# Output projection of a hybrid decoder layer: seven products per 2x2 by 2x2 of tiles in place of eight

## Chip, cores and metric

The kernel runs on one NeuronCore of a Trainium2 chip. The metric is the device time of one execution in microseconds, median of several executions. Engines are named as in the profile: PE (TensorE matmul), PEld (TensorE weight load), DVE (VectorE), ACT (ScalarE), POOL (GpSimd), SP (SyncE, which here issues most loads).

## The reference

One layer on x of 256 tokens by 4096 channels, float32. The change touches the last line but one alone, `merged @ w_out`, a product of 256x4096 by 4096x4096.

```python
h = rms_norm(x, norm_gains[l])
z = h @ w_in[l]                       # all projections at once
...                                   # gated linear attention -> o_a, window attention -> o_b
y_a = (o_a * silu(gg)) @ w_gla_out[l]
y_b = (o_b * silu(sg)) @ w_swa_out[l]
merged = sigmoid(ga + b_gates[l, 0]) * y_a + sigmoid(gb + b_gates[l, 1]) * y_b
x = x + merged @ w_out[l]
...
return rms_norm(x, final_norm_gain)
```

## The kernel before, in words

All large products have one form, the helper `gemm`. The 256 tokens are two tiles (t = 0, 1) of 128 and lie, transposed, as the stationary side; the weights stream as the moving side in blocks of 512 columns; the contraction runs over tiles of 128 rows (KT = 32 of them for 4096). To come near float32, each side is split into a high part, rounded to the type float32r, and a low part, the rest, and three float32r products are added in PSUM: high by high (L136), high by low (L137), low by high (L138). A chunk of two contraction tiles (KW = 2) is one load of 512 KB on SP's queue (L148, `raw`, four buffers), one cast on ScalarE (L154, `hi`) and one subtraction on VectorE (L155, `lo`), both 128x1024, with three buffers each. Then come 12 matmuls (two contraction tiles, two token tiles, three products).

The stages follow each other: the attention branches, `ya` (GLA output projection), eight rounds of the gates `ga`, `gb` and the projection `yb` with the merge into the array `ya`, and last the output projection in eight blocks `o0` to `o7` of 512 columns, with residual, squares for the final norm, and gain. Its stationary side `mT` is `ya` transposed on TensorE (`transpose_split`, L184, tiles `m_t`) and split by ScalarE (L174) and VectorE (L175). Seven of its eight parts are transposed ahead of the last `yb`, the eighth inside `o0`.

Tile pools give out the buffers, and a scheduler lays the instructions of each engine in a fixed order when the kernel is built; the preparation of weights stands in `high_priority`, so it is laid ahead of other work. Each engine runs its order strictly, and waits at an instruction whose inputs or buffers aren't ready.

## Time and profile before

| what | value |
|---|---|
| median of 3 runs | 2497.19 us (2496.21 to 2499.42) |
| span of the profiled execution | 2494.7 us |
| lowest and highest run above that span | 1.5 and 4.7 us |
| PE busy share of the span | 99% |
| VectorE busy share | 52% |
| ScalarE busy share | 44% |
| HBM traffic over the span | 189 GB/s |

The span is what the profiler saw from the first to the last instruction of one execution; the median lies 2.5 us above it. Shares are means over the whole span. The output projection alone is the stretch from 2134.8 to 2484.0 us.

### The profile page before, as it was taken

To read this page: it belongs to the slowest core of one execution; us is meant where nothing else is said; L and a number is where in the kernel's file an instruction comes from. 1 tells how busy PE (TensorE), PEld (TensorE's weight loads), DVE (VectorE), ACT (ScalarE), POOL (GpSimd) and SP (SyncE) were. 2 spreads that over 40 slices of the span, in tenths; PEclk is the share of its full clock that TensorE was granted. 3 is DMA by queue.
4 is the path that set the end of the run, shared out by engine and by line. 5 is a ranking of instruction groups with operands and counts; after the bars stand their busy time and mean duration, and the time that the engine had idled before them with its cause. 6 is when DMAs were issued, how large, how long until landed. Compare 5 with 4: busy or idle time off the path is not lost.

```text
span 2494.7 us, 28744 instructions
## 1 busy us (share of the span) xinstructions
PE 2469.9 (99%) x11220; PEld 2033.3 (82%) x11220; DVE 1306.1 (52%) x1303; ACT 1093.1 (44%) x1289; POOL 41.4 (2%) x52
## 2 busy tenths in 40 slices
PE   8999999999999999999999999999999999999998
PEld 6788888888888888888888888888888888888886
DVE  8565555545444455555555454555545456544544
ACT  6444444434444444544444444444444444444443
POOL 4000000000000000000000000000000000000000
PEclk9999999999999999999999999999999999999999
DMA  7455555445555545454465556665666555665655
GB/s 258 156 175 188 170 175 195 175 168 188 194 192 195 193 148 193 150 171 166 150 211 199 198 198 197 197 202 197 198 196 198 194 194 177 236 211 203 211 203 186
DMA packets 132985, 474.32 MB, mean 190 GB/s; under 512 B 15056, under 2 KB 15440, under 8 KB 132720
## 3 DMA queue, kind: packets, MB, share of 16 engines
q1 hardware_dynamic: 127584, 461.69, 54.5%
q10 hardware_dynamic: 5264, 10.79, 1.4%
q8 instruction: 88, 1.44, 0.2%
q14 instruction: 49, 0.40, 0.0%
HBM read 468.23 MB, written 4.19 MB: 189 GB/s over the span
## 4 chain that ended last, share of the span: by engine, by line
PE 95%; DVE 2%; issue 1%; ACT 1%; DMA 0%; POOL 0%; SPq 0%; ACTq 0%; POOLq 0%; DVEq 0%
PE ga_a L137 5%; PE ga_a L136 5%; PE gb_a L137 5%; PE gb_a L136 5%; PE ga_a L138 5%; PE gb_a L138 5%; PE o_a L136 5%; PE o_a L137 5%; PE o_a L138 5%; PE sg_a L137 2%; PE sg_a L136 2%; PE sg_a L138 2%; PE sq_a L138 2%; PE sq_a L137 2%; PE ya_a L136 2%; PE ya_a L137 2%
## 5 line engine op out<-in xcount | busy, mean ns | idle before, releaser
L155 DVE TENSOR_TENSOR ga_l<-ga_r,ga_h 128x1024 fp32r<-128x1024 f32 x128 | 156.8, 1225 | 171.6 <-ACT ga_h L154 171.6
L155 DVE TENSOR_TENSOR gb_l<-gb_r,gb_h 128x1024 fp32r<-128x1024 f32 x128 | 156.9, 1225 | 171.1 <-ACT gb_h L154 171.1
L155 DVE TENSOR_TENSOR o_l<-o_r,o_h 128x1024 fp32r<-128x1024 f32 x124 | 152.0, 1225 | 161.4 <-ACT o_h L154 161.3
L154 ACT CAST ga_h<-ga_r 128x1024 fp32r<-128x1024 f32 x128 | 135.2, 1057 | 209.8 <-PE ga_a L138 171.5
L154 ACT CAST gb_h<-gb_r 128x1024 fp32r<-128x1024 f32 x128 | 135.2, 1056 | 204.5 <-PE gb_a L138 159.4
L154 ACT CAST o_h<-o_r 128x1024 fp32r<-128x1024 f32 x124 | 131.0, 1056 | 193.2 <-PE o_a L138 186.2
L138 PE MATMUL ga_a<-ga_h,hT 128*128 128x512 f32 x512 | 199.4, 389 | 0.0
L137 PE MATMUL ga_a<-ga_l,hT 128*128 128x512 f32 x512 | 199.2, 389 | 0.0
L136 PE MATMUL ga_a<-ga_h,hT 128*128 128x512 f32 x512 | 199.2, 389 | 0.0
L138 PE MATMUL gb_a<-gb_h,hT 128*128 128x512 f32 x512 | 199.2, 389 | 0.0
L136 PE MATMUL gb_a<-gb_h,hT 128*128 128x512 f32 x512 | 199.2, 389 | 0.0
L137 PE MATMUL gb_a<-gb_l,hT 128*128 128x512 f32 x512 | 199.2, 389 | 0.0
L138 PE MATMUL o_a<-o_h,mT 128*128 128x512 f32 x496 | 193.0, 389 | 0.0
L137 PE MATMUL o_a<-o_l,mT 128*128 128x512 f32 x496 | 193.0, 389 | 0.0
L136 PE MATMUL o_a<-o_h,mT 128*128 128x512 f32 x496 | 192.9, 389 | 0.0
L155 DVE TENSOR_TENSOR ya_l<-ya_r,ya_h 128x1024 fp32r<-128x1024 f32 x64 | 78.4, 1226 | 95.6 <-ACT ya_h L154 95.6
L155 DVE TENSOR_TENSOR sq_l<-sq_r,sq_h 128x1024 fp32r<-128x1024 f32 x64 | 78.4, 1225 | 84.8 <-ACT sq_h L154 84.8
L155 DVE TENSOR_TENSOR yb_l<-yb_r,yb_h 128x1024 fp32r<-128x1024 f32 x64 | 78.4, 1225 | 82.8 <-ACT yb_h L154 82.8
L155 DVE TENSOR_TENSOR gg_l<-gg_r,gg_h 128x1024 fp32r<-128x1024 f32 x64 | 78.3, 1224 | 75.9 <-ACT gg_h L154 75.9
L155 DVE TENSOR_TENSOR sg_l<-sg_r,sg_h 128x1024 fp32r<-128x1024 f32 x64 | 78.3, 1223 | 72.7 <-ACT sg_h L154 72.7
L154 ACT CAST sg_h<-sg_r 128x1024 fp32r<-128x1024 f32 x64 | 67.4, 1053 | 111.0 <-PE sg_a L138 94.7
L155 DVE TENSOR_TENSOR gv_l<-gv_r,gv_h 128x1024 fp32r<-128x1024 f32 x64 | 78.2, 1224 | 67.9 <-ACT gv_h L154 67.9
(278 smaller groups left out, 5568.3 us busy)
## 6 DMA issues: line engine op xcount, KB each, us to landing
ga_r<-in_win_dram SPq DMA_DIRECT2D x128, 512.0 KB, 4.3
gb_r<-in_win_dram SPq DMA_DIRECT2D x128, 512.0 KB, 4.2
o_r<-in_wout_dram SPq DMA_DIRECT2D x128, 512.0 KB, 3.3
gv_r<-in_win_dram SPq DMA_DIRECT2D x64, 512.0 KB, 3.2
gg_r<-in_win_dram SPq DMA_DIRECT2D x64, 512.0 KB, 3.3
ya_r<-in_wgla_dram SPq DMA_DIRECT2D x64, 512.0 KB, 3.2
sq_r<-in_win_dram SPq DMA_DIRECT2D x64, 512.0 KB, 3.2
sg_r<-in_win_dram SPq DMA_DIRECT2D x64, 512.0 KB, 3.3
```

Source lines behind the costliest of these rows:

```text
L136: nc.tensor.matmul(acc[t], lh, hi[:, i, :], start=kt == 0, stop=False)
L137: nc.tensor.matmul(acc[t], lh, lo[:, i, :], start=False, stop=False)
L138: nc.tensor.matmul(acc[t], ll, hi[:, i, :], start=False, stop=kt == nkt - 1)
L154: nc.scalar.copy(hi, raw)
L155: nc.vector.tensor_tensor(lo, raw, hi.bitcast(F32), ALU.subtract)
```

## The change

The output projection is computed by the scheme of seven products (Winograd's form of Strassen's). One unit, numbered j = 0 to 15 within a block, takes two contraction tiles, two token tiles and two blocks of 512 columns at once, so there are four blocks of 1024 columns (named `o0`, `o2`, `o4`, `o6` in the code) of 16 units each. One load of 1 MB (L569, `raw`, two buffers) brings the four weight tiles of a unit, laid out for it by the host. Of the seven products of a unit three (q1, q2, q3) are one plain float32 matmul each, with the unsplit tiles on both sides (L602); the other four are three float32r matmuls each (L598 to L600) on sums of weight tiles. The sums are made on VectorE (L571, 128x1024 into `t13`; L589 and L590, 128x512 into `t24`), split by ScalarE (L578) and VectorE (L579), 128x1024 for each pair. The seven results gather over the 16 units in seven PSUM banks and are combined by VectorE at the block's end (L630 to L637), followed by residual, squares and gain (L622 within `done`).

The transposes of `ya` all move behind the last `yb`: `combine(j)` transposes four 128x128 tiles into the eighth PSUM bank (one buffer, `tp`), ScalarE copies them out, VectorE makes four sums of 128x128 (L552 to L555), ScalarE casts and VectorE subtracts 128x512 (L557, L558). The pools of the earlier stages are closed first, and the new tiles lie where those tiles lay.

```diff
 STG = 3
+NFULL = 3
+T13 = 1
+BUFS = {"13": 2, "24": 2}
...
-            if n == NBLK - 1:
-                mT = big.tile([P, KT, 2, S], F32R, tag="hT", name="mT")
-                for m in range(n):
-                    merged(m)
...
-        for n in range(NBLK):
-            cs = slice(n * NB, (n + 1) * NB)
-            xt = fp.tile([P, NT, NB], F32, tag="xt", name=f"xt{n}", bufs=2)
...
-            acc = gemm(
-                f"o{n}", mT, wout[n], KT,
-                before=(lambda k0, _: merged(NBLK - 1) if k0 == 8 else None) if n == 0 else None,
-                trail=STG + 4 if n == NBLK - 1 else 0, hold=hold,
-            )
...
+    early.close()
...
+    def combine(j):
...
+        tp = qps.tile([P, 512], F32, tag="tp", name=f"m_t{j}")
+        for k in range(2):
             for t in range(NT):
...
+                nc.tensor.transpose(tp[:, k * S + t * P : k * S + (t + 1) * P], ya[:, t, c : c + P], ident)
+        tv = tp.rearrange("p (k t c) -> p k t c", k=2, t=NT)
+        cs = fp.tile([P, 6, P], F32, tag="cs", name=f"cs{j}", bufs=2)
+        nc.scalar.copy(fl[:, 0:2, :], tv[:, :, 0, :])
+        nc.scalar.copy(cs[:, 0:2, :], tv[:, :, 1, :])
...
+        nc.vector.tensor_tensor(cs[:, 2, :], cs[:, 0, :], cs[:, 1, :], ALU.subtract)
+        nc.vector.tensor_tensor(cs[:, 4, :], fl[:, 0, :], cs[:, 0, :], ALU.subtract)
+        nc.vector.tensor_tensor(cs[:, 3, :], cs[:, 2, :], fl[:, 0, :], ALU.subtract)
+        nc.vector.tensor_tensor(s4, fl[:, 1, :], cs[:, 3, :], ALU.add)
+        c = cs[:, 1 : 8 - NFULL, :]
+        nc.scalar.copy(sp_[:, :, 0, :], c)
+        nc.vector.tensor_tensor(sp_[:, :, 1, :], c, sp_[:, :, 0, :].bitcast(F32), ALU.subtract)
...
+    def sevens(name, w, npr):
...
+        q = {i: qps.tile([P, NB], F32, tag=f"q{i}", name=f"{name}_q{i}") for i in range(1, 8)}
+        for j in range(npr):
+            with tc.high_priority(PRIO):
+                raw = wp.tile([P, 4, NB], F32, tag="raw", name=f"{name}_r{j}", bufs=2)
+                nc.sync.dma_start(raw, w[j])
+                t13 = wp.tile([P, 2, NB], F32, tag="t13", name=f"{name}_t{j}", bufs=T13)
+                nc.vector.tensor_tensor(
+                    t13, raw[:, 0:2, :], raw[:, 2:3, :].broadcast_to([P, 2, NB]), ALU.add
+                )
...
+                    nc.scalar.copy(hi, src)
+                    nc.vector.tensor_tensor(lo, src, hi.bitcast(F32), ALU.subtract)
...
+                t24 = wp.tile([P, 2, NB], F32, tag="t24", name=f"{name}_s{j}")
+                nc.vector.tensor_tensor(t24[:, 0, :], t13[:, 1, :], raw[:, 0, :], ALU.add)
+                nc.vector.tensor_tensor(t24[:, 1, :], t24[:, 0, :], raw[:, 3, :], ALU.add)
...
+            order = (1, 6, 5, 3, 2, 7, 4) if j == npr - 1 else (1, 2, 3, 5, 7, 6, 4)
...
+                    nc.tensor.matmul(q[i], l[:, 0, :], hi, start=st, stop=False)
+                    nc.tensor.matmul(q[i], l[:, 0, :], lo, start=False, stop=False)
+                    nc.tensor.matmul(q[i], l[:, 1, :], hi, start=False, stop=sp_)
+                else:
+                    nc.tensor.matmul(q[i], full[j // GRP][:, j % GRP, FULL[i], :], right[i], start=st, stop=sp_)
...
+        nc.scalar.copy(u, q[1])
+        add(v, q[6], u)
+        add(y, q[5], v, ALU.subtract)
+        add(x2[:, 0, cs[1]], q[3], y)
+        add(x2[:, 0, cs[0]], q[2], u)
+        add(w, q[7], v)
+        add(x2[:, 1, cs[1]], q[5], w, ALU.subtract)
+        add(x2[:, 1, cs[0]], q[4], w)
+        for t, i in ((0, 1), (0, 0), (1, 1), (1, 0)):
+            done(t, i)
```

What the build lays on the engines, at the places that the prediction speaks of. First TensorE at the end of the last `yb` (L136 to L138 before, L140 to L142 now), where the output projection begins. Before:

```order
L136 MATMUL yb_a_15026<-yb_h_15155,obT 128x512
L137 MATMUL yb_a_15026<-yb_l_15156,obT 128x512
L138 MATMUL yb_a_15026<-yb_h_15155,obT 128x512
L136 MATMUL o_a_15185<-o_h_15189,mT 128x512
L137 MATMUL o_a_15185<-o_l_15190,mT 128x512
```

And now, at the same place:

```order
L140 MATMUL yb_a_14927<-yb_h_15056,obT 128x512
L141 MATMUL yb_a_14927<-yb_l_15057,obT 128x512
L142 MATMUL yb_a_14927<-yb_h_15056,obT 128x512
L546 MATMUL m_t_15103<-ident,ya 128x128 x4
L546 MATMUL m_t_15117<-ident,ya 128x128 x4
L546 MATMUL m_t_15131<-ident,ya 128x128 x4
L602 MATMUL o_q_15331<-o_r_15338,full_15093 128x512
```

Three of the sixteen groups of transposes now stand between the last `yb` and the first product; the others are strewn over the first block. The first two loads of the output projection on SP's queue, with the semaphores that they wait for, before and now:

```order
L148 DMA o_r_15187<-in_wout_dram 128x1024 [waits DMAHW6_49,DVE_49]
L148 DMA o_r_15205<-in_wout_dram 128x1024 [waits DMAHW7_49,DVE_49]
```

```order
L569 DMA o_r_15338<-in_wout_dram 128x2048 [waits PE_49]
L569 DMA o_r_15368<-in_wout_dram 128x2048 [waits DMAHW1_49,DMAHW0_49,DVE_49]
```

The first load waited for VectorE's use of a staging buffer; now it waits for TensorE, to a count that the last matmul of the last `yb` reaches, since its tile lies where `obT` lay. Second, VectorE in the middle of a block, before (the whole preparation of three chunks is three rows):

```order
L155 TENSOR_TENSOR o_l_16224<-o_r_16221,o_h_16223 128x1024
L155 TENSOR_TENSOR o_l_16242<-o_r_16239,o_h_16241 128x1024
L155 TENSOR_TENSOR o_l_16260<-o_r_16257,o_h_16259 128x1024
L155 TENSOR_TENSOR o_l_16278<-o_r_16275,o_h_16277 128x1024
L155 TENSOR_TENSOR o_l_16296<-o_r_16293,o_h_16295 128x1024
```

And now (o_t is `t13`, o_s is `t24`, o_l_13 with o_t the low part of `t13`, with o_s that of `t24`):

```order
L571 TENSOR_TENSOR o_t_16245<-o_r_16243 128x1024
L589 TENSOR_TENSOR o_s_16251<-o_t_16245,o_r_16243 128x512
L590 TENSOR_TENSOR o_s_16251<-o_s_16251,o_r_16243 128x512
L579 TENSOR_TENSOR o_l_13_16248<-o_t_16245,o_h_13_16247 128x1024
L579 TENSOR_TENSOR o_l_13_16255<-o_s_16251,o_h_13_16254 128x1024
L571 TENSOR_TENSOR o_t_16275<-o_r_16273 128x1024
```

Two chunks of before are one unit now: two rows of 1024 have become three of 1024 and two of 512. Third, VectorE in the first block, where the sums of the transposed side (L552 to L558) stand among the preparation of the weights:

```order
L579 TENSOR_TENSOR o_l_9_15613<-o_t_15610,o_h_9_15612 128x1024
L590 TENSOR_TENSOR o_s_15616<-o_s_15616,o_r_15608 128x512
L552 TENSOR_TENSOR cs_15234<-cs_15234 128x128
L553 TENSOR_TENSOR cs_15234<-full_15095,cs_15234 128x128
L554 TENSOR_TENSOR cs_15234<-cs_15234,full_15095 128x128
L552 TENSOR_TENSOR cs_15248<-cs_15248 128x128
L555 TENSOR_TENSOR full_15095<-full_15095,cs_15234 128x128
L553 TENSOR_TENSOR cs_15248<-full_15095,cs_15248 128x128
L579 TENSOR_TENSOR o_l_9_15620<-o_s_15616,o_h_9_15619 128x1024
L558 TENSOR_TENSOR split_15099<-cs_15234,split_15099 128x4x128
```

The same work stood ahead of and beside the last `yb` before, as one cast and one subtraction of 128x512 for two contraction tiles.

## Rows read from the trace of the kernel before

**Rows 1.** The page: busy time of each engine (share of the span), and the chain of work that ended last, by engine.

```profile
PE 2469.9 (99%) x11220; PEld 2033.3 (82%) x11220; DVE 1306.1 (52%) x1303; ACT 1093.1 (44%) x1289; POOL 41.4 (2%) x52
...
PE 95%; DVE 2%; issue 1%; ACT 1%; DMA 0%; POOL 0%; SPq 0%; ACTq 0%; POOLq 0%; DVEq 0%
```

**Rows 2.** The busy time by stretch: the output projection, and what follows it. Columns: the stretch and its length, each engine's busy time and instructions, the granted TensorE clock (1.00 is full speed), DMA share, GB/s.

```profile
core 0: us, PE busy (x) PEld busy (x) DVE busy (x) ACT busy (x) POOL busy (x), PEclk, DMA share, GB/s
2134.80:2484.00 349.20, 349.20 (x1545) 288.91 (x1543) 177.14 (x166) 145.42 (x160) 0.55 (x1) 1.00 0.60 209
2484.00:2494.70 10.70, 0.02 (x1) 0.00 (x0) 2.82 (x6) 2.91 (x4) 0.56 (x1) 0.63 0.57 223
```

**Rows 3.** Groups of instructions in the stretch 2134.8 to 2484.0: line, engine, operation, output and inputs, shapes, count | busy us, mean ns of one | idle before, and what ended it.

```profile
L138 PE MATMUL o_a<-o_h,mT 128*128 128x512 f32 x496 | 193.0, 389 | 0.0
...
L155 DVE TENSOR_TENSOR o_l<-o_r,o_h 128x1024 fp32r<-128x1024 f32 x122 | 149.5, 1225 | 158.4 <-ACT o_h L154 158.4
L154 ACT CAST o_h<-o_r 128x1024 fp32r<-128x1024 f32 x122 | 128.9, 1056 | 189.9 <-PE o_a L138 186.2 <-PE yb_a L138 1.7 <-DMA o_r<-in_wout_dram 1.6
...
L545 DVE TENSOR_TENSOR x<-o_a,xt 128x512 f32<-128x512 f32 x15 | 9.7, 683 | 5.5 <-PE o_a L138 5.5
...
L548 DVE TENSOR_TENSOR x<-x,gf 128x512 f32<-128x512 f32 x14 | 9.0, 685 | 0.0
...
L184 PE MATMUL m_t<-ident,ya 128*128 128x128 f32 x8 | 1.0, 273 | 0.0
```

**Rows 4.** TensorE in order of time, where the last `yb` ends (start us, duration us, engine, line, operation).

```profile
2134.55 0.39 PE L138 MATMUL yb_a<-yb_h,obT 128*128 128x512 f32 x1
2134.77 0.39 PE L136 MATMUL o_a<-o_h,mT 128*128 128x512 f32 x1
2135.00 0.39 PE L137 MATMUL o_a<-o_l,mT 128*128 128x512 f32 x1
```

**Rows 5.** TensorE in order of time: plain float32 products of 256 columns in the linear attention. One product of the code is two instructions here (x2).

```profile
163.24 0.59 PE L366 MATMUL op<-v,ats 128*128 128x256 f32 x2
163.68 0.59 PE L367 MATMUL op<-v,ats 128*128 128x256 f32 x2
164.11 0.33 PE L345 MATMUL at<-qs,ks 128*128 128x64 f32 x2
```

**Rows 6.** VectorE in order of time around the start of the output projection.

```profile
2134.48 1.28 DVE L523 TENSOR_TENSOR sgm<-yb_a,sgm 128x512 f32<-128x512 f32 x2
2135.68 0.68 DVE L524 TENSOR_TENSOR ya<-ya,sgm 128x512 f32<-128x512 f32 x1
2136.28 1.22 DVE L155 TENSOR_TENSOR o_l<-o_r,o_h 128x1024 fp32r<-128x1024 f32 x1
2137.42 0.68 DVE L524 TENSOR_TENSOR ya<-ya,sgm 128x512 f32<-128x512 f32 x1
```

**Rows 7.** VectorE in order of time: two sums of 256 columns that follow each other.

```profile
214.81 0.75 DVE L388 TENSOR_TENSOR gt<-oraw,gt 128x256 f32<-128x256 f32 x2
```

**Rows 8.** VectorE in order of time: an instruction that needs the result of the one ahead of it (L287 of L284).

```profile
122.33 1.22 DVE L155 TENSOR_TENSOR gv_l<-gv_r,gv_h 128x1024 fp32r<-128x1024 f32 x1
123.47 0.69 DVE L284 TENSOR_SCALAR l<-l 128x1024 f32<-128x1024 f32 x1
124.19 0.69 DVE L287 TENSOR_TENSOR_SCAN b<-cmask,l 128x256 f32<-128x256 f32 x1
```

**Rows 9.** TensorE in order of time at the transposes of `ya`, and then the same transposes counted over the whole run (count, shortest, median and longest ns, first and last start).

```profile
2106.30 0.39 PE L138 MATMUL gb_a<-gb_h,hT 128*128 128x512 f32 x1
2106.53 1.91 PE L184 MATMUL m_t<-ident,ya 128*128 128x128 f32 x16
2108.20 0.48 PE L136 MATMUL yb_a<-yb_h,obT 128*128 128x512 f32 x1
```

```profile
L184 PE MATMUL m_t<-ident,ya x64: 270/272/328, 2106.5 to 2146.4; 128*128 128x128 f32 x64
```

**Rows 10.** Loads issued in the output projection: count, KB each, median us from issue to landing.

```profile
o_r<-in_wout_dram SPq DMA_DIRECT2D x121, 512.0 KB, 3.3
xt<-in_x_dram ACTq DMA_DIRECT2D x8, 512.0 KB, 4.8
```

**Rows 11.** The same view for the first loads of the kernel (8 to 28 us), when the DMA engines are fully used: packets and rate, and time to landing.

```profile
DMA packets 1902, 6.87 MB, mean 343 GB/s; under 512 B 225, under 2 KB 225, under 8 KB 1902
...
gq_r<-in_win_dram SPq DMA_DIRECT2D x6, 512.0 KB, 5.9
```

**Rows 12.** All engines in order of time after the last product (2484.02 us is its end): residual, square, sum, power, scaling. The span ends at 2494.7.

```profile
2484.06 0.69 DVE L545 TENSOR_TENSOR x<-o_a,xt 128x512 f32<-128x512 f32 x1 [4.98 <-PE o_a L138]
2484.78 0.63 ACT L546 ACTIVATE xt<-x 128x512 f32<-128x512 f32 x1 [5.32 <-DVE x L545]
...
2485.54 0.16 DVE L551 TENSOR_REDUCE sf<-st 128x1 f32<-128x8 f32 x1 [0.79 <-ACT xt L546]
...
2485.97 0.56 POOL L90 TENSOR_TENSOR sf<-sf,mhalf 128x1 f32<-128x1 f32 x1 [8.73 <-DVE sf L89]
2486.56 2.19 ACT L562 ACTIVATE x<-x,sf 128x1024 f32<-128x1024 f32 x2 [1.05 <-POOL sf L90]
```

**Rows 13.** ScalarE in order of time: two casts of 128x1024 that follow each other.

```profile
137.21 1.98 ACT L154 CAST gv_h<-gv_r 128x1024 fp32r<-128x1024 f32 x2
```

More of the change, by code (lines that the diff above doesn't have):

```diff
@@ L389, in trunk_kernel @@
                 transpose_split(oaT, pi * 4, gt, 4, f"oa{pi}")
-    late = ctx.enter_context(tc.tile_pool(name="late", bufs=1))
+    late = ctx.enter_context(tc.tile_pool(name="late", bufs=1, side="right"))
     ya = late.tile([P, NT, DM], F32, tag="ya", name="ya")
@@ new lines, in trunk_kernel @@
+    early.close()
+    NPR = KT // 2
+    hp = ctx.enter_context(tc.tile_pool(name="hp", bufs=1, reuse_waits="tile"))
+    wp = ctx.enter_context(tc.tile_pool(name="wp", bufs=1, reuse_waits="tile"))
+    fp = ctx.enter_context(tc.tile_pool(name="fp", bufs=1, reuse_waits="tile"))
+    qps = ctx.enter_context(
+        tc.tile_pool(name="qps", bufs=1, space=bass.MemoryType.PSUM, reuse_waits="tile")
+    )
+    GRP = 4
+    full = [hp.tile([P, GRP, NFULL, P], F32, name=f"full{g}") for g in range(NPR // GRP)]
@@ new lines, in trunk_kernel @@
+    for t in range(NT):
+        sf = fp.tile([P, 1], F32, name=f"sf{t}")
+        nc.vector.tensor_reduce(sf, st[:, t, :], AX.X, ALU.add)
+        rms_scale(sf, sf, DM)
+        for c in range(4):
+            os = slice(c * 1024, (c + 1) * 1024)
+            if c % 2 == 0:
+                nc.vector.tensor_scalar(x2[:, t, os], x2[:, t, os], sf, None, ALU.mult)
+            else:
+                nc.scalar.activation(x2[:, t, os], x2[:, t, os], AF.Copy, scale=sf)
+            nc.sync.dma_start(out[t * P : (t + 1) * P, os], x2[:, t, os])
```

89 lines of the change are left out of this document (55 added, 34 removed).

## The prediction, as it was put on record

> **What bounds the kernel now.** I read the page's busy shares and its chain first [rows 1]: TensorE is busy for 99% of the span and holds 95% of the chain that ended last, so time is won or lost by what TensorE has to do and by how often something else makes it wait. Then the stage that changes, alone [rows 2]: 349.2 us, TensorE busy throughout at full clock, VectorE 177 us, ScalarE 145 us. Then its groups [rows 3]: VectorE's subtraction waits 158 us for ScalarE's cast, and the cast waits 186 us for TensorE, which frees the buffers. Both are idle for half of the stage because they are ahead; TensorE alone sets the pace. The eight transposes there take 0.9 us (0.109 us each, below), which leaves 348.3 us for 1536 products, 0.2268 us from start to start, as consecutive starts show too [rows 4]. The duration of 389 ns that the groups give is a latency; spacing is what counts. The profiled span is 2494.7 us and the median 2497.2: I take 2.5 us as lying around it.
>
> **TensorE's price for a unit.** A unit of the new scheme replaces 24 float32r products, 24 x 0.2268 = 5.44 us. Twelve remain: 2.72 us. The three plain float32 products have no row of 512 columns. The nearest are the 256-column ones [rows 5]: each is two instructions, and the pairs start 0.44 and 0.43 us apart, so 0.435 us for a product and 0.87 us for twice the columns. Bounds: 0.435 if columns beyond 256 cost nothing, 0.91 if each of four passes costs as much as a float32r product. I take 0.87, hence 2.72 + 2.61 = 5.33 us, 85.3 us for a block of 16 units. The gain is 0.11 us per unit, 7 us in all: three plain products cost nearly what the nine split ones did plus the three of the eighth product.
>
> The Trainium skill (page "FP8 and Floating Point Precision", section "TensorE Precision Notes") says that true float32 takes four passes through the array; at four times 0.2268 us a plain product would be 0.91 us and the result about 5 us later. By the row it is 0.87, four passes of 0.109 us at 256 columns, so the trace agrees with the count of passes and makes them slightly cheaper.
>
> **VectorE's price for a unit.** Instructions that follow each other without waiting start 1.14 us apart for 1024 columns and 0.60 for 512 [rows 6]. Two of 256 take 0.75 together [rows 7]; a duration exceeds a spacing by 0.08 us in rows 6, so that spacing is 0.33, and the line through the three gives 0.20 for 128. An instruction that needs the result just ahead of it starts 0.03 us after its end instead of 0.08 before [rows 8], 0.12 us later. Before, two chunks cost VectorE 2 x 1.14 = 2.3 us per 5.44. Now a unit has three of 1024 (one sum, two low parts) and two of 512: 3 x 1.14 + 2 x 0.60 = 4.62 us, and 4.85 where the two sums follow the first directly. Its spare time falls from 3.1 us to 0.5 per unit. ScalarE's two casts, 0.93 us apart [rows 13] (1.98 for two, less one duration of 1.06), are 2 us and stay hidden: a cast with its hand-overs is some 1.17 us after the first sum, while VectorE makes two sums in 1.3.
>
> **The start of the stage.** The transposes that stood ahead of and within the last `yb` are now behind it. From the first of them to the first output product there are 28.24 us [rows 9, 4], of which 96 `yb` products take 96 x 0.2268 = 21.77; so the stage begins 6.5 us earlier. But its first load now waits for the last `yb` product, and was hidden under `yb` before. A load of 512 KB lands in 3.3 us [rows 10]; the second half adds 0.52 MB at 343 GB/s [rows 11], 1.5 us: 4.8 us (bounds 3.3, and 6.6 for two landings). Meanwhile come the merge's last sums and two rounds of transposes, copies and sums. VectorE starts on the first unit about 5.5 us into the stage; before, TensorE went on without a gap [rows 4].
>
> **The first block.** VectorE also makes the sums of the transposed side: four of 128 columns and one of 512, 4 x 0.20 + 0.60 plus one dependence, 1.5 us for each of the 14 rounds that remain. It needs 16 x 4.62 + 14 x 1.5 = 94.9 us; TensorE needs 85.3 + 52 x 0.109 = 91. VectorE is the bound. I add 2.5 us for its waits on casts that stand behind copies in ScalarE's order, 3.5 us for the next block's first sums, which stand ahead of the last low part of the left side, and 0.9 us for the four products that need this: 5.5 + 94.9 + 2.5 + 3.5 + 0.9 = 107.3 us.
>
> **The other blocks.** Within a block TensorE sets the pace again, 5.33 against 4.85. At a block's end VectorE has 15 more instructions of 512 columns, 9.0 us (seven of the recombination, four residuals, four gains), laid among six units. In these it gains 6 x (5.33 - 4.62) = 4.3 us. How far it can be ahead is set by the two load buffers: a load for unit j + 2 may start when q3 of unit j is done, 2.6 us into that unit, lands at 7.6, and with sums and splits the last low part is there at 7.6 + 1.26 + 0.72 + 0.60 + 1.14 + 1.23 = 12.6; TensorE wants it at 2 x 5.33 + 2.61 + 7 x 0.2268 = 14.9. So 2.3 us are covered, and 9.0 - 4.3 - 2.3 = 2.4 us of stall remain per block. The second block has its first product behind it: 85.3 - 0.9 + 2.4 = 86.8; the last two take 87.7 each. Stage: 107.3 + 86.8 + 175.4 = 369.5 us against 349.2, 20.3 us more.
>
> **The end.** Before, 10.7 us from the last product to the end of the span [rows 2, 12]: one residual sum, one square, the power (1.02 us from reduction to scaling), two scalings on ScalarE (2.19), and 5.95 us for the stores and what follows. Eight blocks left one token tile to finish; now both tiles and both column halves end together. From v, 0.6 us ahead of the last product's end, VectorE has twelve instructions of 0.60 and a dependence until the first reduction (6.7 us), 1.0 to the scaling, two scalings of 0.67, the second reduction and power (1.0), two on ScalarE: 6.7 + 1.0 + 1.3 + 1.0 + 2.2 = 12.2, and 5.95 behind: 18.2 us, 7.5 more.
>
> **Sum.** 20.3 + 7.5 - 6.5 = +21.3 us: span 2516.0, time 2518.5, which I round to 2519, slower by 0.9%. A measurement can tell some 0.2%, 5 us, from no change.
>
> **Rivals.** (1) *VectorE loses time in every unit.* Its order is strict: a cast that comes late, or a load that lands later than 4.8 + 2.3 = 7.1 us, holds the sums, low parts and recombination queued behind. For this speak its narrow spare time (0.5 us) and that loads under full use of the DMA engines take 5.9 us [rows 11]; against it, the 3.3 us in this stage [rows 10]. It decides once the waits pass 0.48 us per unit. At 0.75 the last 48 units lose 0.27 each, 13 us, and the first 16 lose 12 - 2.5 = 9.5: 2541. (2) *Not slower: VectorE's sums are cheaper and stay hidden.* TENSOR_SCALAR of 1024 columns takes 0.69 us where a TENSOR_TENSOR takes 1.22 [rows 8]. If the three sums of a unit ran at that rate, VectorE would need about 3.6 us, 5.1 with the transposed side, against TensorE's 5.33: it decides once that is below TensorE's price. Then the first block is 5.5 + 91, the others 85.3: 352.4, and the time 2497.2 + 3.2 + 7.5 - 6.5 = 2501, within the bound. Against it: every TENSOR_TENSOR row here has the slow rate.
>
> The Trainium skill (page "VectorE: DVE Perf Modes", section "The perf-mode tier table (the rule you actually need)") gives `tensor_tensor` on float32 the single rate only and `tensor_scalar` the double one. The trace agrees with both (1.22 and 0.69 us), and by it this rival falls and the sum stays.
>
> (3) *Faster: that, and cheap plain products.* At 0.435 us each a unit costs TensorE 4.08 us, the stage about 300, the time about 2450. Cheap products alone win nothing: the blocks then wait for VectorE's 16 x 4.85 + 9.0 = 87 us each. Against it speaks that a product's price grows with its columns [rows 5].
>
> **Chances.** The forecast 0.61 (its own range 2508 to 2530: waits, load and first block at their bounds), rival 1 0.22, rival 2 0.11, rival 3 0.06. Leaving out rivals 2 and 3 and the outer edge of rival 1, the range is 2503 to 2541. Slower 0.83, within 0.2% 0.11, faster 0.06.
>
> **What would show it.** Plain products starting 0.43 us apart per instruction, two for each; VectorE over 90% busy in the first block, with TensorE's waits there ended by VectorE's low parts; a gap of some 5 us behind the last `yb`; TensorE near 100% in the middle of later blocks, with 2 to 3 us of waits at each block's start; 18 us behind the last product. I am wrong if VectorE's sums take other than 1.14 and 0.60 us, if loads of 1 MB land past 7 us, or if TensorE's clock falls with its waits, which a granted clock under 1.00 in the stage would tell.

## The result

The changed kernel takes 2533.68 us (median of 3 runs, 2532.66 to 2535.49) and the kernel before 2497.19 us: a ratio of 1.0146, 95% interval 1.0128 to 1.0164. It is 1.5% slower where 0.9% was forecast. The profiled execution has a span of 2530.9 us, 36.2 longer than before; the forecast's sum was 21.3. So the direction held and 15 us are to be found.

The page's line of busy times and its chain, which answer to [rows 1]:

```profile
PE 2478.4 (98%) x10836; PEld 1961.8 (78%) x10836; DVE 1483.7 (59%) x1587; ACT 1104.6 (44%) x1325; POOL 42.1 (2%) x52
...
PE 89%; DVE 5%; DMA 2%; issue 1%; ACT 1%; POOL 0%; SPq 0%; ACTq 0%; POOLq 0%; DVEq 0%
```

VectorE and the DMA engines have entered the chain. Where, the busy time by stretch shows (it answers to [rows 2]; the columns are those named there). The stretches are: last `yb` product to the second block, the second, third and fourth block, the end.

```profile
core 0: us, PE busy (x) PEld busy (x) DVE busy (x) ACT busy (x) POOL busy (x), PEclk, DMA share, GB/s
2129.60:2238.63 109.03, 100.50 (x353) 60.88 (x352) 104.49 (x170) 55.04 (x83) 0.00 (x0) 0.97 0.49 179
2238.63:2328.05 89.42, 86.62 (x289) 53.47 (x288) 84.65 (x93) 35.91 (x40) 0.00 (x0) 1.00 0.57 206
2328.05:2418.06 90.01, 87.50 (x289) 53.38 (x288) 84.93 (x95) 36.73 (x41) 0.00 (x0) 1.00 0.58 207
2418.06:2508.24 90.18, 87.02 (x289) 53.29 (x287) 84.45 (x96) 35.69 (x40) 0.00 (x0) 1.00 0.53 190
2508.24:2530.90 22.66, 0.16 (x1) 0.00 (x0) 11.20 (x22) 7.26 (x12) 1.40 (x2) 0.54 0.47 185
```

Against the forecast's terms:

| term | forecast | measured | difference |
|---|---|---|---|
| last `yb` product to second block | 107.3 | 109.0 | +1.7 |
| second, third, fourth block | 86.8, 87.7, 87.7 | 89.4, 90.0, 90.2 | +7.4 |
| end (behind the last product) | 18.2 | 22.5 | +4.3 |
| start of the stage | -6.5 | -5.2 | +1.3 |

The end counts from 2508.40, where the last product is shown to end, as 10.7 did from 2484.02 [rows 12]; the table's differences add up to 14.7, the rest is rounding.

TensorE in order of time at the start and inside the third block:

```profile
2107.60 0.39 PE L142 MATMUL gb_a<-gb_h,hT 128*128 128x512 f32 x1
...
2129.36 0.39 PE L142 MATMUL yb_a<-yb_h,obT 128*128 128x512 f32 x1
...
2134.71 4.51 PE L602 MATMUL o_q<-o_r,full 128*128 128x512 f32 x6 [0.94 <-DMA o_r<-in_wout_dram]
...
2340.43 2.73 PE L602 MATMUL o_q<-o_r,full 128*128 128x512 f32 x6
2342.60 0.79 PE L598 MATMUL o_q<-o_h,split 128*128 128x512 f32 x1
```

From the last `gb` product to the last `yb` one there are 21.76 us, before 2134.55 - 2106.30 = 28.25 [rows 4, 9]: the stage comes 6.49 us earlier, as forecast. The 1.3 us that are missing lie ahead of it: the last `gb` product itself is 1.3 us later (2107.60 against 2106.30). At 2340.43 six instructions, three plain products, take 2.73 us: five spacings and one duration of 0.59, so the spacing is 0.429 us and a product costs 0.857.

The same row at 2134.71 takes 4.51 us for as many instructions. The busy time by stretch gives the granted clock there, and behind a wait of 2.2 us at the end of the first block:

```profile
2134.70:2137.00 2.30, 2.29 (x3) 1.11 (x4) 2.23 (x3) 1.14 (x2) 0.00 (x0) 0.52 1.03 406
...
2234.00:2238.00 4.00, 4.00 (x11) 3.00 (x11) 4.00 (x7) 1.04 (x1) 0.00 (x0) 0.60 0.00 0
```

0.52 is the lower of the two levels, 1.2 GHz: after 5.1 us of mostly waiting TensorE worked at half pace for 3.5 us, four of the six instructions.

Now the loads. SyncE, VectorE and TensorE in order of time, first in the third block's first units, then in the middle of the second block (L569 is the load, its row counts three and starts with the first; L571 the sum of 1024 columns, L590 the second dependent sum, which reads the loaded tile last; L622 a residual sum and a gain):

```profile
2342.74 0.68 DVE L590 TENSOR_TENSOR o_s<-o_s,o_r 128x512 f32<-128x512 f32 x1
2343.34 1.22 DVE L571 TENSOR_TENSOR o_t<-o_r 128x1024 f32<-128x1024 f32 x1
2343.48 11.96 SPq L569 DMA_DIRECT2D o_r<-in_wout_dram  x3
...
2344.47 0.69 DVE L622 TENSOR_TENSOR x<-x,xt 128x512 f32<-128x512 f32 x1
...
2347.95 0.68 DVE L622 TENSOR_TENSOR x<-x,gf 128x512 f32<-128x512 f32 x1
2348.55 0.68 DVE L590 TENSOR_TENSOR o_s<-o_s,o_r 128x512 f32<-128x512 f32 x1
2349.15 1.22 DVE L571 TENSOR_TENSOR o_t<-o_r 128x1024 f32<-128x1024 f32 x1
```

```profile
2305.99 0.69 DVE L590 TENSOR_TENSOR o_s<-o_s,o_r 128x512 f32<-128x512 f32 x1
2306.61 2.73 PE L602 MATMUL o_q<-o_r,full 128*128 128x512 f32 x6
...
2309.38 0.33 SPq L569 DMA_DIRECT2D o_r<-in_wout_dram  x1
```

In the middle of a block the last plain product ends at 2309.34 and the load starts 0.04 us later: TensorE frees the buffer, as the forecast had it. Behind a block's start it is VectorE: its second sum ends at 2343.42 and the load starts at 2343.48. From the first sum of that unit to the end of its last are 2343.34 to 2349.23, 5.9 us, since a residual sum and a gain of the block before stand between them: with these two VectorE needs 4.62 + 2 x 0.60 = 5.82 us for a unit. The three loads of the row (11.96 us) are 5.81 apart, while TensorE's price for a unit is 5.29. So VectorE frees the buffer for units 3 to 7 of the second block, 4 to 11 of the third and 3 to 11 of the fourth (at unit 11 VectorE is the later one by less than 0.1 us).

In the third block the loads of the gains and the residual are in the way (ScalarE's queue and VectorE in order of time; then, of the tile's own view for 2364 to 2370, the time from issue to landing):

```profile
2362.11 0.35 ACTq L611 DMA_DIRECT2D gf<-in_gfin_dram  x1
...
2372.84 1.22 DVE L571 TENSOR_TENSOR o_t<-o_r 128x1024 f32<-128x1024 f32 x1 [1.37 <-DMA o_r<-in_wout_dram]
```

```profile
DMA to landing us min/median/max: 7.0/7.0/7.0
```

The load for unit 8 takes 7.0 us instead of 4.8, and so it does in the fourth block; in the second the load for unit 7 takes 7.5. This is called the collision below. At the end, ScalarE and SyncE in order of time, then what the DMA engines moved behind the last product, after and before:

```profile
2516.89 2.19 ACT L649 ACTIVATE x<-x,sf 128x1024 f32<-128x1024 f32 x2 [1.16 <-POOL sf L94]
...
2518.07 7.90 SPq L650 DMA_DIRECT2D out_dram<-x  x8
...
2519.23 2.19 ACT L649 ACTIVATE x<-x,sf 128x1024 f32<-128x1024 f32 x2 [0.15 <-POOL sf L94]
```

```profile
DMA packets 1152, 4.19 MB, mean 186 GB/s; under 512 B 128, under 2 KB 128, under 8 KB 1152
```

```profile
DMA packets 886, 2.38 MB, mean 223 GB/s; under 512 B 112, under 2 KB 112, under 8 KB 886
```

The last scaling ends at 2521.42, 13.0 us behind the last product; 9.4 us follow, where 5.95 were forecast from [rows 12]. Before, 1.8 of the 4.2 MB had gone out while TensorE still worked. Behind the first store the DMA engines move some 400 GB/s until less than 2 us before the end.

### The profile page after: what moved, and what is told of

Same layout as the page of the kernel before. It is cut to its first block, busy times and chain, and to the rows that moved or that the text cites. A ratio compares the mean times of both kernels' runs of the same rounds, so it can differ in the third digit from the quotient of the medians.

```text
span 2530.9 us, 28092 instructions
## 1 busy us (share of the span) xinstructions
PE 2478.4 (98%) x10836; PEld 1961.8 (78%) x10836; DVE 1483.7 (59%) x1587; ACT 1104.6 (44%) x1325; POOL 42.1 (2%) x52
## 3 DMA queue, kind: packets, MB, share of 16 engines
HBM read 468.23 MB, written 4.19 MB: 187 GB/s over the span
## 4 chain that ended last, share of the span: by engine, by line
PE 89%; DVE 5%; DMA 2%; issue 1%; ACT 1%; POOL 0%; SPq 0%; ACTq 0%; POOLq 0%; DVEq 0%
PE ga_a L140 5%; PE gb_a L140 5%; PE ga_a L142 5%; PE ga_a L141 5%; PE gb_a L142 5%; PE gb_a L141 5%; PE o_q L602 4%; PE sg_a L141 2%; PE sg_a L140 2%; PE sg_a L142 2%; PE sq_a L141 2%; PE sq_a L140 2%; PE ya_a L141 2%; PE gg_a L142 2%; PE yb_a L140 2%; PE yb_a L142 2%
## 5 line engine op out<-in xcount | busy, mean ns | idle before, releaser
L142 PE MATMUL ga_a<-ga_h,hT 128*128 128x512 f32 x512 | 199.4, 389 | 0.0
L140 PE MATMUL ga_a<-ga_h,hT 128*128 128x512 f32 x512 | 199.2, 389 | 0.0
L140 PE MATMUL gb_a<-gb_h,hT 128*128 128x512 f32 x512 | 199.2, 389 | 0.0
L142 PE MATMUL gb_a<-gb_h,hT 128*128 128x512 f32 x512 | 199.2, 389 | 0.0
L602 PE MATMUL o_q<-o_r,full 128*128 128x512 f32 x384 | 189.1, 601 | 8.9 <-DMA o_r<-in_wout_dram 8.5
L598 PE MATMUL o_q<-o_h,split 128*128 128x512 f32 x256 | 121.3, 502 | 4.9 <-ACT split L557 2.2
L602 PEld LDWEIGHTS o_q<-o_r,full 128*128 128x128 f32 x384 | 71.6, 190 | 59.4 <-issue 31.1
L599 PE MATMUL o_q<-o_l,split 128*128 128x512 f32 x256 | 113.9, 445 | 0.5 <-DVE o_l L579 0.5
L158 ACT CAST gg_h<-gg_r 128x1024 fp32r<-128x1024 f32 x64 | 67.5, 1054 | 103.6 <-PE gg_a L142 87.6
```

What stands on the lines that cost most here:

```text
L140: nc.tensor.matmul(acc[t], lh, hi[:, i, :], start=kt == 0, stop=False)
L142: nc.tensor.matmul(acc[t], ll, hi[:, i, :], start=False, stop=kt == nkt - 1)
L158: nc.scalar.copy(hi, raw)
L598: nc.tensor.matmul(q[i], l[:, 0, :], hi, start=st, stop=False)
L599: nc.tensor.matmul(q[i], l[:, 0, :], lo, start=False, stop=False)
L602: nc.tensor.matmul(q[i], full[j // GRP][:, j % GRP, FULL[i], :], right[i], start=st, stop=sp_)
```

## The experiments

One measure serves for all of them: how far TensorE is behind its own price. It is a product's start, less the first output product's, less the price of everything between (0.2268 us for a float32r product, 0.857 for a plain one, 0.109 for a transpose), read behind 16, 32, 48 and 64 units:

| kernel | 16 | 32 | 48 | 64 | time, us (ratio to before) |
|---|---|---|---|---|---|
| changed | 13.2 | 18.3 | 23.2 | 29.1 | 2533.68 (1.0146) |
| the same again | 13.8 | 18.8 | 23.4 | 28.0 | 2530.55 (1.0133) |
| third load buffer | 11.1 | 14.1 | 17.7 | 19.0 | 2522.93 (1.0101) |
| dependent sums on GpSimd | 39.5 | 71.7 | 103.9 | 137.5 | 2639.25 (1.0567) |
| sums left out | 3.1 | 3.9 | 4.4 | 5.0 | 2506.88 (1.0039) |
| first token tile finished first | 14.6 | 20.2 | 24.6 | 33.2 | 2533.17 (1.0136) |
| gains and residual loaded once | 10.1 | 13.6 | 17.8 | 23.1 | 2527.57 (1.0123) |
| residual and gains left out | 12.2 | 15.6 | 18.1 | 20.6 | 2518.91 (1.0086) |
| first load ahead of the stage | 8.1 | 17.0 | 20.2 | 26.3 | 2530.38 (1.0134) |
| sums first | 8.0 | 13.7 | 27.9 | 34.7 | 2537.31 (1.0160) |
| three edits together | 13.4 | 15.6 | 17.0 | 18.4 | 2515.06 (1.0073) |

The intervals of the ratios are 0.0015 to 0.002 to either side; the blocks are those of one profiled execution each.

The same measure within a block, as what the first four units, the next four and the last eight add (second, third and fourth block; a unit is counted as 18 of TensorE's instructions):

| kernel | units 0 to 3 | units 4 to 7 | units 8 to 15 |
|---|---|---|---|
| changed | 2.3, 1.9, 3.0 | 2.5, 2.1, 2.0 | 0.4, 0.9, 0.8 |
| the same again | 2.2, 1.9, 2.9 | 2.5, 1.9, 0.1 | 0.4, 0.7, 1.5 |
| third load buffer | 2.6, 3.2, 0.9 | 0.2, 0.1, 0.1 | 0.3, 0.2, 0.2 |
| gains and residual loaded once | 2.3, 3.1, 3.4 | 0.6, 0.2, 0.3 | 0.5, 0.9, 1.7 |
| residual and gains left out | 2.9, 1.9, 1.9 | 0.1, 0.1, 0.1 | 0.4, 0.4, 0.5 |

**The changed kernel again.**

> The changed kernel once more, to see how much of a block's length differs from one execution to another: blocks of 104, 89.4, 90.0 and 90.2 us to within 1 us each if they are set by the program, and the last `yb` product between 2128 and 2130 us.

The blocks took 104.6, 89.3, 89.6 and 88.9 us, the last `yb` product started at 2127.7 and the end was as long: the blocks agree to within 1.3 us, not the 1 expected, and the start lies 0.3 us ahead of what was expected: it moves by more than a microsecond from one execution to another. Of the forecast's 15 us, the 1.3 at the start are of this kind. The collision isn't there each time either: here the fourth block's load for unit 8 landed after 4.95 us, with the gains' and the residual's loads issued as long before it as in the first execution, and units 4 to 7 add 0.1.

**A third load buffer.**

```diff
-                raw = wp.tile([P, 4, NB], F32, tag="raw", name=f"{name}_r{j}", bufs=2)
+                raw = wp.tile([P, 4, NB], F32, tag="raw", name=f"{name}_r{j}", bufs=3)
...
-        y = fp.tile([P, NB], F32, tag="y", name=f"y{n}")
-        w = fp.tile([P, NB], F32, tag="w", name=f"w{n}")
+        y = x2[:, 1, cs[0]]
+        w = fp.tile([P, NB], F32, tag="u", name=f"w{n}")
```

> A third buffer for the loaded tile of 1 MB; to make room, y is kept in x2's still unwritten columns and w takes u's place (same instructions). Theory A, the load's release: in the profile of the changed kernel each load of the first eight units of blocks 2 to 4 is issued 0.06 us after VectorE's second dependent sum of two units earlier, lands 4.8 us later, and VectorE and TensorE then wait for it; a third buffer takes that wait away, and blocks 2 to 4 fall from 89.4, 90.0 and 90.2 us to 85 to 87 each, the whole to 2519 to 2526 us. Theory B, VectorE's own work (95% busy there) sets these blocks: they stay within 1 us, the whole at 2530 to 2536. By both the first block stays near 104 and the end near 22.5.

The span fell to 2519.0. The second to fourth block by stretch:

```profile
2237.05:2323.95 86.90, 85.16 (x289) 53.95 (x288) 85.45 (x95) 36.55 (x41) 0.00 (x0) 1.00 0.58 212
2323.95:2412.21 88.26, 86.03 (x290) 54.07 (x289) 87.34 (x99) 36.98 (x42) 0.00 (x0) 1.00 0.58 208
2412.21:2498.20 85.99, 85.45 (x289) 53.86 (x287) 81.40 (x93) 34.48 (x40) 0.00 (x0) 1.00 0.53 189
```

89.4, 90.0 and 90.2 became 86.9, 88.3 and 86.0, 8.5 us of the 11.9 gained, with the same work on VectorE: theory A. Nearly all of it goes from units 4 to 7, although loads for unit 8 still take 8.1 and 7.9 us in the third and fourth block: they start early enough. The third block keeps more than it expected (VectorE is busy for 99% of it). The end fell to 20.8, which neither theory had: VectorE's order there came out otherwise, as it did with the sums left out, and the first store came 8.0 us behind the last product instead of 9.8. The first block is 2.1 us shorter, which needn't be the buffer's: the edit also moves y, w and where the tiles lie, and the first loads of gains and residual now go out at 1269 and 1271 us instead of 2131 and 2132. No run moved these alone.

**The dependent sums on GpSimd.**

```diff
-                nc.vector.tensor_tensor(t24[:, 0, :], t13[:, 1, :], raw[:, 0, :], ALU.add)
-                nc.vector.tensor_tensor(t24[:, 1, :], t24[:, 0, :], raw[:, 3, :], ALU.add)
+                nc.gpsimd.tensor_tensor(t24[:, 0, :], t13[:, 1, :], raw[:, 0, :], ALU.add)
+                nc.gpsimd.tensor_tensor(t24[:, 1, :], t24[:, 0, :], raw[:, 3, :], ALU.add)
```

> The two dependent sums of 512 columns go from VectorE to GpSimd, which is idle in the stage. Theory B (VectorE's work is the bound, and the only one): VectorE needs 1.3 us less per unit, the first block falls from 104 to 92 to 96 and the others to 85 to 87; the whole to 2508 to 2518. Rival: the two engines slow each other (in the first 40 us of the trace a VectorE subtraction of 1024 columns takes up to 2.16 us instead of 1.21 while GpSimd adds 512 columns, which takes it 1.32 to 2.3 us): the first block stays above 100 and the whole above 2528. If theory A holds as well, the later second sum (two of at least 1.3 us instead of 0.6) holds the loads back further, and blocks 2 to 4 don't fall below 88.

2639.25 us (1.0567): far past the rival. The groups of VectorE and GpSimd in the output projection:

```profile
L579 DVE TENSOR_TENSOR o_l<-o_t,o_h 128x1024 fp32r<-128x1024 f32 x64 | 90.6, 1415 | 49.1 <-ACT o_h L578 49.1
L579 DVE TENSOR_TENSOR o_l<-o_s,o_h 128x1024 fp32r<-128x1024 f32 x64 | 78.4, 1225 | 111.7 <-ACT o_h L578 111.6
...
L590 POOL TENSOR_TENSOR o_s<-o_s,o_r 128x512 f32<-128x512 f32 x64 | 128.5, 2008 | 5.0
```

The engines do slow each other: the low part that runs beside a GpSimd sum takes 1.42 us instead of 1.22, and GpSimd's second sum 2.0. The Trainium skill (page "SBUF — State Buffer", section "SBUF: two separate sides") says that VectorE operations with two inputs in SBUF and GpSimd operations take a shared pair of ports in turn, the loser waiting for the whole instruction; the trace agrees that they hinder each other, though most of the loss is not that. VectorE now idles 161 us ahead of its low parts, because its order is strict: weight sum (1.2), two GpSimd sums (1.3 and 2.1, each 0.1 behind what it waits for), cast (1.05), low part (1.2), and only then the next unit's weight sum: 7.1 us for each unit in the middle of a block, 117 for a block. This answers nothing about theory A: the chain is longer than any load.

**The four sums left out.**

```diff
-                t13 = wp.tile([P, 2, NB], F32, tag="t13", name=f"{name}_t{j}", bufs=T13)
-                nc.vector.tensor_tensor(
-                    t13, raw[:, 0:2, :], raw[:, 2:3, :].broadcast_to([P, 2, NB]), ALU.add
-                )
+                t13, t24 = raw[:, 0:2, :], raw[:, 2:4, :]
...
-                t24 = wp.tile([P, 2, NB], F32, tag="t24", name=f"{name}_s{j}")
-                nc.vector.tensor_tensor(t24[:, 0, :], t13[:, 1, :], raw[:, 0, :], ALU.add)
-                nc.vector.tensor_tensor(t24[:, 1, :], t24[:, 0, :], raw[:, 3, :], ALU.add)
```

> Leaves out the four weight sums of a unit (the split products take the loaded tiles in their place), so that VectorE has two low parts of 1024 columns per unit, 2.3 us against TensorE's 5.3, and the loaded tile waits for no sum. It shows TensorE's price alone: 12 float32r products at 0.227 and three plain ones at 0.857 are 5.29 us a unit, 84.7 a block, 90.4 for the first with its transposes. If everything above this is VectorE's sums and the waits they bring (theories A and B together): blocks 84.7 to 85.5, first block 91 to 94, start and end as in the changed kernel (5.3 and 22.5), the whole 2507 to 2512. Rival, the plain products themselves cost more where they meet float32r products or loads: the blocks stay above 87 and the whole above 2517.

The blocks came as expected; the end, expected unchanged at 22.5, is 20.7. The whole is 2506.88 us, 0.1 under the range, the first block 93.5, and the others are by stretch

```profile
2227.83:2313.25 85.42, 85.42 (x290) 53.99 (x289) 46.98 (x48) 35.21 (x41) 0.00 (x0) 1.00 0.59 215
2313.25:2398.51 85.26, 85.26 (x289) 54.06 (x288) 46.98 (x48) 35.27 (x41) 0.00 (x0) 1.00 0.60 216
2398.51:2483.80 85.29, 85.29 (x289) 53.88 (x287) 46.97 (x49) 33.67 (x40) 0.00 (x0) 1.00 0.57 203
```

TensorE is busy for the whole of each, at 85.3 us against 16 x 24 x 0.2268 = 87.1 before. So all that TensorE gains is 1.8 us a block (by its price of 5.29 us a unit it would be 2.4), and all but 5 of the 29 us behind its price are the sums' and what waits on them. Even with the sums free the kernel stays 0.4% slower: the gap at the start (5.1 us), the transposes within the first block and the longer end (20.7) take more than the gain.

**The first token tile finished first.**

```diff
+        last = n == NBLK - 2
+        if last:
+            done(0, 1)
+            done(0, 0)
+            finish(0)
         add(w, q[7], v)
         add(x2[:, 1, cs[1]], q[5], w, ALU.subtract)
         add(x2[:, 1, cs[0]], q[4], w)
-        for t, i in ((0, 1), (0, 0), (1, 1), (1, 0)):
+        for t, i in ((1, 1), (1, 0)) if last else ((0, 1), (0, 0), (1, 1), (1, 0)):
             done(t, i)
+    finish(1)
```

(`finish(t)` is the loop over token tiles that ends the kernel, for one of them.)

> In the last block the first token tile is finished, scaled and stored before the second one is recombined; same instructions. Theory, the stores: the end of 22.5 us is 4.2 MB of stores behind the first scaled columns, at some 400 GB/s, so the time from the first store to the end (12.8 us) stays and the first store is 1.8 to 2.4 us earlier: the end is 20.1 to 20.7 us. Rival: the chain on VectorE and ScalarE to the last scaling sets the end; that chain is as long as before, and the end stays at 22 to 23. The blocks are as in the changed kernel; the whole 2531 to 2532 or 2533 to 2534.

```profile
2519.13 7.96 SPq L617 DMA_DIRECT2D out_dram<-x  x8
```

Counted from 0.23 us behind the last product's start, SyncE's first store is 1.74 us earlier (8.09 against 9.83), and the end 1.75 us shorter (20.87 against 22.62), although the last scaling ends at 2524.99, 13.95 us behind that instead of 13.2. From the first store to the end are 12.78 us; they are 12.79 in the changed kernel and 12.78 or 12.79 with the third buffer and without the sums (13.1 to 13.2 in three later kernels). So the end is the stores' transfer behind the first store, 4.19 MB, and not the chain of scalings. The whole took 2533.17 us (1.0136), no difference: the fourth block was 2.7 us longer in the profile. There the load for its unit 8 took 7.7 us, behind the residual's and the gains' loads, and was not caught up.

**Gains and residual loaded once.**

```diff
-        gf_ = fp.tile([P, 2 * NB], F32, tag="gf", name=f"gf{n}")
-        nc.scalar.dma_start(gf_, gfin[n * NB : (n + 2) * NB].partition_broadcast(P))
-        xt = fp.tile([P, NT, 2 * NB], F32, tag="xt", name=f"xt{n}")
-        nc.scalar.dma_start(xt, x[:, n * NB : (n + 2) * NB].rearrange("(t p) c -> p t c", p=P))
+        if n == 0:
+            gf_ = fp.tile([P, 2 * NB], F32, tag="gf", name=f"gf{n}")
+            nc.scalar.dma_start(gf_, gfin[n * NB : (n + 2) * NB].partition_broadcast(P))
+            xt = fp.tile([P, NT, 2 * NB], F32, tag="xt", name=f"xt{n}")
+            nc.scalar.dma_start(xt, x[:, n * NB : (n + 2) * NB].rearrange("(t p) c -> p t c", p=P))
```

> Leaves out the loads of the residual and the gains (1.5 MB) of blocks 2 to 4, which take those of the first. In the profile of the changed kernel the load for unit 8 of blocks 3 and 4 lands 7.0 us after its issue instead of 4.8 while these transfers run, and the units behind it wait. Theory: this collision costs some 2 us in each of the three blocks: they fall to 87 to 88 us, the whole to 2526 to 2529. Rival: the lateness is made good by VectorE's spare time in the second half of the block (0.5 us a unit), and the blocks stay at 89 to 90.

2527.57 us (1.0123), the blocks 88.1, 88.9 and 89.6: the total as the theory had it, the blocks between the two. Units 4 to 7 add 0.6, 0.2 and 0.3 us instead of 2.5, 2.1 and 2.0: the collision costs some 1.9 us where it happens. The units around them add more than in the changed kernel, and half of the gain is gone. The first block, which the edit doesn't touch, was 3 us shorter in this execution; that part of the gain is not the edit's, and a difference of that size in a first block says little in the other runs.

**Residual and gains left out.**

```diff
             o, xi = x2[:, t, cs[i]], xt[:, t, i * NB : (i + 1) * NB]
-            add(o, o, xi)
             nc.scalar.activation(xi, o, AF.Square, accum_out=st[:, t, n + i : n + i + 1])
-            add(o, o, gf_[:, i * NB : (i + 1) * NB], ALU.mult)
```

> Leaves out the residual sums and gains, eight of the 15 instructions of 512 columns (4.8 us) that VectorE has at a block's end; their loads stay, two load buffers as in the changed kernel. By the forecast's own working the rest, 4.2 us, is covered by VectorE's gain of 4.3 us in six units: no stall but the collision of unit 8's load (some 2 us). Theory, the recombination stretches the time from the first weight sum to the second dependent one (5.9 us in the units after a block's start, 5.0 later) and so holds back both loads and sums: blocks 2 to 4 fall to 86 to 87.5 us. Rival, the loads alone are too slow for two buffers whatever VectorE does in between: the blocks stay at 89 to 90. By both the end is 4.8 us shorter, 17.8, since the first store is that much earlier. The whole: 2518 to 2523 by the theory, 2527 to 2530 by the rival.

```profile
2237.61:2325.34 87.73, 85.86 (x289) 53.83 (x288) 83.27 (x89) 36.25 (x41) 0.00 (x0) 1.00 0.56 201
2325.34:2412.48 87.14, 85.92 (x290) 53.92 (x289) 83.00 (x88) 36.83 (x41) 0.00 (x0) 1.00 0.56 205
2412.48:2499.70 87.22, 86.00 (x289) 53.71 (x287) 81.82 (x88) 35.82 (x40) 0.00 (x0) 1.00 0.54 192
```

2518.91 us (1.0086). With two buffers 7.5 us go from the three blocks (87.7, 87.1 and 87.2, at the theory's upper edge), and the end is 17.1 us. TensorE frees the buffers for units 4 to 11 again, and their loads land after 4.7 to 5.0 us. So loads of 1 MB are not too slow for two buffers by themselves. But the run changes two things at once. Nothing reads the gains any more, so that their loads for the later blocks all go out in the first (2139 to 2149 us), and the residual's load is over before that for unit 7 starts: the collision is gone as well. What the run gains stands in units 4 to 7, where the run before, with VectorE's work as it was, gains nearly as much. So most of what these units lose takes both, a load that starts late behind VectorE's queue and one that lands late by the collision, and this run doesn't part them. Against the theory, and against the forecast's working, the first four units lose 2.9, 1.9 and 1.9 us, about as before, although VectorE has 4.8 us less to do there.

**The first load ahead of the stage.**

```diff
-    hp = ctx.enter_context(tc.tile_pool(name="hp", bufs=1, reuse_waits="tile"))
     wp = ctx.enter_context(tc.tile_pool(name="wp", bufs=1, reuse_waits="tile"))
+    hp = ctx.enter_context(tc.tile_pool(name="hp", bufs=1, reuse_waits="tile"))
```

> The pool of the loaded tiles is opened before that of the left side, so that its first buffer lies where the norm's input lay and not where the last `yb` products still read: the first load waits for the last `gb` product, 22 us earlier, and is there when the stage begins. Theory, the load alone makes the gap: the gap between the last `yb` product and the first output product (5.1 us) falls to 2.3 to 3.0 us, what is left being merge, transposes, copies and left-side sums; the first block gains no more than 1 us beside it, since VectorE, which sets that block, starts its first weight sum only after the left-side sums of two rounds, 0.4 us earlier than now: the next block starts 0.5 to 1.5 us earlier, the whole 2532 to 2533. Rival, the gap is lost time one for one: the whole is 2.5 us or more shorter, and more if the granted clock, 0.83 behind the gap, stays at 1.00.

```profile
2133.16 0.66 PE L546 MATMUL m_t<-ident,ya 128*128 128x128 f32 x4 [1.53 <-ACT cs L550]
2133.66 3.60 PE L602 MATMUL o_q<-o_r,full 128*128 128x512 f32 x8
```

2530.38 us (1.0134). The gap fell from 5.1 to 4.0 us only, less than the theory said: the load was there, but TensorE's order has three rounds of transposes ahead of the first product, and the last waits for the copies that empty their only PSUM tile. That wait was hidden behind the load's. VectorE's first weight sum came 1.2 us earlier, not 0.4, and the products behind the gap start 0.43 us apart: the clock stayed at 1.00 here. Counted from the last `yb` product, the kernel is 6.2 us ahead of the changed one behind 16 units, 2.1 behind 20 and 3.9 at the last product: the second block gives back most of what the first gained, for which no run gives a cause. The total, 3 us less than the changed kernel's with an interval of 4 to either side, decides nothing, and the changed kernel's second execution has 2530.55 too.

**The sums first.**

```diff
-                right[5], right[7] = parts("13", t13, 2)
                 t24 = wp.tile([P, 2, NB], F32, tag="t24", name=f"{name}_s{j}")
                 nc.vector.tensor_tensor(t24[:, 0, :], t13[:, 1, :], raw[:, 0, :], ALU.add)
                 nc.vector.tensor_tensor(t24[:, 1, :], t24[:, 0, :], raw[:, 3, :], ALU.add)
+                right[5], right[7] = parts("13", t13, 2)
                 right[6], right[4] = parts("24", t24, 2)
```

> The two dependent sums stand right behind the first one in the program, ahead of both casts and low parts, so that a load's buffer is free of VectorE earlier; two buffers as in the changed kernel. In the order that comes out VectorE makes 13 of the 15 instructions of the recombination between the second and third unit of a block. Theory A (the load's release) would give part of what the third buffer gave: blocks 2 to 4 at 86 to 88.5 us, the whole 2524 to 2530. Rival: 9 us of VectorE's work in one piece is more than the two units made ahead cover, and TensorE waits for it once per block: blocks at 90 to 93, the whole 2533 to 2542.

2537.31 us (1.0160), the rival in the total. The first block, which has no recombination ahead of it, fell from 109.0 to 103.8 us; the others took 90.4, 98.5 and 91.5. In the third one wait brings another; TensorE in order of time:

```profile
2327.78 0.40 PE L600 MATMUL o_q<-o_h,split 128*128 128x512 f32 x1
2332.09 2.07 PE L602 MATMUL o_q<-o_r,full 128*128 128x512 f32 x2 [3.91 <-DVE x L622]
...
2335.09 0.63 PE L599 MATMUL o_q<-o_l,split 128*128 128x512 f32 x1
2335.52 0.63 PE L600 MATMUL o_q<-o_h,split 128*128 128x512 f32 x1
```

After 3.9 us of waiting for a recombination sum that frees a PSUM tile, float32r products start 0.43 us apart instead of 0.227 until 2338. The place of the recombination in VectorE's order mattered more here than when a buffer comes free.

**Three edits together**: third buffer, first load ahead of the stage, first token tile finished first.

> Three edits together: the third load buffer, the first load ahead of the stage, the first token tile finished first. If the three costs are separate, the span is that of the third buffer alone (2519.0) less 1 to 2.5 us at the start and 1 to 2 us at the end: the whole 2518 to 2521, still 0.8% above the kernel before. If the third buffer has already given what the other two would, it stays at 2522 to 2524.

2515.06 us (1.0073, interval 1.0056 to 1.0089), better than either expectation. The span is 5.7 us under that of the third buffer alone: 2.8 at the end (17.95 us), 1.2 in the gap (3.9), 0.2 in the blocks, of which the last three are now 86.5, 86.0 and 86.1 and the first 2.4 longer behind the gap, and 1.5 that lie ahead of the stage and are the execution's. So the gap and the end are costs of their own. It is still slower than the kernel before, as the one without the sums is.

## Why the prediction was right in direction and short in size

2533.68 us lies in the stated range, 2503 to 2541, but above the forecast's own, 2508 to 2530, in the part that only rival 1 reached. Rival 1 is not what the rows show: it had VectorE lose 0.27 us in every unit, and the losses stand in the first eight units of a block, with 0.4 to 0.9 us in the eight behind them.

**TensorE's price: right.** Two instructions 0.429 us apart for a plain product, 0.857 us (forecast 0.87), and 5.29 us for a unit (5.33). The Trainium skill's four passes (page "FP8 and Floating Point Precision", section "TensorE Precision Notes") would be 0.91 by four times 0.2268, an estimate; the row is 0.857, so the trace fits the count at a price 5% lower, and the forecast was right to take the row. (Rival 3's 4.08 us for a unit should be 2.72 + 3 x 0.435 = 4.03.)

**VectorE's price: right.** Weight sums take 1.22 and 0.68 us, as in [rows 6]; followed at once by other work they start 1.14 and 0.60 apart, at the single rate. Rival 2 falls, and rival 3 with it.

**Start and gap: right**, -6.49 us (forecast -6.5) and 5.1 (5.5); the load landed in 4.8. That the gap is the load's was half wrong: with the load out of the way 4.0 us remain, the transposes' own.

**First block: right**, 109.0 against 107.3, VectorE busy for 104.5 of it. The run without sums shows it directly: 13.2 us behind TensorE's price become 3.1. One sign failed: TensorE's waits were to end with VectorE's low parts. Behind the gap the view of waits names 5.7 us, 2.8 ended by loads, 2.2 by a cast of the left side and 0.5 by its low part; none by a low part of the weights. And the close match holds some luck, since the same work took 103.8 us with the sums first. The clock fell here, which the forecast named as a way to be wrong; it lies almost wholly beside VectorE's work, so that it can't have cost much, but no run shows its price alone.

**The other blocks: wrong by 7.4 us.** The step that failed is "a load for unit j + 2 may start when q3 of unit j is done". It holds in the second half of a block and not for units 4 to 7 or 4 to 11, where VectorE's second dependent sum reads the tile last and residual sums and gains stand ahead of it. For unit 8 of the third block that is 2365.72 against 2363.65 for TensorE's last plain product, 2.1 us. Also missed was the collision, 2.2 us more for the same load: rival 1 named loads past 7.1 us as the point from which they cost time, and the rows show 7.0 to 7.7 there, at most once per block and not in every unit. The two together exceed the cover of 2.3 us that the two buffers were to give. (By its own terms the load would land at 2.6 + 4.8 = 7.4 and not 7.6, and the cover be 2.5.) Taking away the collision, or giving the lead of a third buffer, brings what units 4 to 7 lose from 2.2 us to 0.1 to 0.6. What was forecast as 2.4 us of stall is 5 to 6.

The forecast's 2.4 us themselves seem to be there, as the 2.3, 1.9 and 3.0 us of the first four units, but the agreement looks like luck. By the forecast's sum they would be gone with 4.8 us of VectorE's work; without the residual sums and gains they are 2.9, 1.9 and 1.9.

**The end: wrong by 4.3 us.** The chain to the last scaling was nearly right (13.0 us behind the last product, forecast 12.2). The step that failed is "5.95 behind": it was taken from a kernel that had stored most of its first token tile before the last product, so that 2.4 MB were left; now 4.2 MB are, 12.8 us from the first store although the chain behind it ends 0.8 us later in one run.

**How to read the waits:** the view of waits names only 8.5 us for TensorE in the second to fourth block, while it falls 15.9 behind its price there; the rest is products that start late by less than the view counts as idle.

What stays open are the last 6 us of the second to fourth block with three buffers (7.9 behind TensorE's price, 1.9 without sums). Nearly all of them, 6.7 us, are lost in the blocks' first four units, and neither the third buffer, nor the transfers left out, nor 4.8 us less of VectorE's work takes them away. TensorE's waits there end with a cast, a load, a low part or a recombination sum, so the cause stays open; only leaving out the weight sums removed it.

## What to carry to other kernels

Before two buffers are counted as lead, list every reader of the buffer and put the last one in its engine's order: a buffer that a matrix product frees in one stretch is freed in another by an elementwise engine that is behind. And price a load beside the other transfers of its stretch: 4.8 us alone became up to 7.7 beside 1.5 MB of others. Fewer products are worth only what their price falls by: here one of eight was saved, three others became plain, and the products became 64 x 0.15 = 9.6 us cheaper, while the sums and what waits on them cost 24, a gap 5, the transposes that moved into the stage 5 and an end that begins with all of the output unstored 12. When outputs become ready all at once, price the end from the first store and the bytes that are left, not from the last computed tile.
